# A transformer layer whose expert stage mixes dense products and row gathers: 64 of its 384 dense tokens change sides for the first table

## The chip, the cores and the metric

The kernel runs on one core of one Trainium2 chip. The metric is the device time of one execution in microseconds (us). The engines are TensorE (PE, with its weight loads shown apart as PEld), VectorE (DVE), ScalarE (ACT), GpSimd (POOL) and SyncE (SP, which only issues transfers here); 16 DMA engines move the data.

## The reference, cut to what matters

One layer for 512 latent tokens of width 1024: an attention and gated-delta sublayer, then PEER, a retrieval of single-neuron experts. There are 16384 experts; each token takes 16 of them in each of 8 heads, 128 in all.

```python
s = einsum('phxd,xkd->phxk', q, sub_keys)          # scores against 2 x 128 keys
s_top, i_top = top_k(s, 16)                        # per head and half
cand = s_top[:, :, 0, :, None] + s_top[:, :, 1, None, :]
best, pos = top_k(cand, 16)
expert = i1 * 128 + i2                             # 16 experts per head
gate = softmax(best)
act = gelu(einsum('phkd,pd->phk', u_tab[expert], xt))
y = einsum('phk,phkd->pd', gate * act, v_tab[expert])
```

The tables u_tab and v_tab have 16384 rows of 1024 float32 values, 64 MB each.

## The kernel before, in words

The first part (to about 540 us) computes the mixing sublayer and is not touched. What follows is written in `_peer`. The 512 tokens lie in four slots of 128.

Slots 0 to 2 (ND = 384 tokens) are dense. The 16384 experts are taken in 128 blocks of 128. For each block `t_uload` loads 512 KB of the U table, `t_usplit` (L2099 on ACT, L2101 on DVE) splits it into two float16 halves, `t_u` multiplies it with all 384 tokens (24 matmuls of 384 columns, named 128x384 in the profile), and `t_act` (L2134) takes the Gelu into an activation block. `t_g` (L2190, L2195, L2197) multiplies the block with the gates and splits the product, `t_vsplit` (L2174, L2176) splits 512 KB of the V table, and `t_v` accumulates the output (18 matmuls of 512 columns, 128x512).

The gates of the dense tokens come from `t_gates`: each slot's ranking (`t_top`, `t_slot`) leaves 128 pairs of keys and a gate per token; transposes (L1995), one-hot rows built by DVE (L2023 to L2029, four operations for 16 tokens, 24 such chunks) and small matmuls (128x128) make a full matrix of gates, which ACT copies out (L2041) and a transfer writes to DRAM as `wd` (L2046). `ev_wall` is set when all 24 chunks are written. Only then are `wd` and the V table read, so no product with V can begin before it.

Until then an activation block has to be kept. The blocks come from `acts`: 8 (`acts0`) and 21 (`actsq`) and 6 (`acts1`) before the gates are done, 16 more after. When none is free and `ev_wall` is not set, `t_u` may use one of two spill buffers and park the block in DRAM (`actd`, L2138), at most NSPILL = 20 times; `t_aload` (L2151) reads these back after the wall.

Slot 3 (GSLOT) gathers. `t_gather` (L2267) waits for the slot's ranking and for the wall, and for each of 128 picks gathers 128 rows of U (512 KB, one row for each token); `t_gu` (L2277, two DVE instructions) takes the dot products. Then 128 gathers of V follow, which `t_gv` (L2299) scales and sums. Four row buffers (`grow`) go round, and gather n is held back until dense block (n - 4) * 32 / 100 has its gates.

The order on each engine is fixed when the program is built: every task is a generator with a priority (a lower number goes first), and a planner with a cost for each instruction always takes the ready step that can begin earliest, within a small window the one of the lowest number. U splits have 60.5, the slots' ranking 61 to 61.7, gates 70, 71 and 72 by slot, U and V loads 74 and 73, slot 3's ranking 75.5, gathers 77, their products 78, V products 81. The engines then run their queues in that order and wait on semaphores.

Of the kernel before, what the change touches and what calls it, by code (L numbers as in the profile page):

```python
# [16 lines left out]
F32 = mybir.dt.float32  # L17
# [138 lines left out]
def get(res, n=1):  # L156
    return ("get", res, n)
# [22 lines left out]
def ac(n, p=0, sb=0):  # L180
    return ("ACT", 0.051 + 0.042 * sb + n * 0.833e-3 + 0.093 * p)
# [1512 lines left out]
def _peer(nc, V, A, G, PE, io, dbg, drv, sync, mm, reg, bk, bc, Bump, gp4, at3, obk, h2hl, h2d, x1d, modrow, dp_,  # L1694
          sm, cst, ident, TILE, ev_h2, ev_gdn, ev_attall, ev_odone, stats, bnhalf, moments, fetch):

    ND = 384
    NE = 128
    NCH = ND // 16
    US, GS = 64.0, 16.0  # L1700
# [31 lines left out]
    h2g = reg(170.5, [D])  # L1732
    scr = reg(152.5, [D], BF16)
    ya = [reg(37 + 4 * i, [D]) for i in range(2)]
    grow = Res([reg(69 + 4 * i, [D]) for i in range(4)])
    ust = Res([reg(17 + 4 * i, [KT, 128]) for i in range(3)])
    uhl = Res([(reg(29 + 4 * i, [KT, 128], F16), reg(31 + 4 * i, [KT, 128], F16)) for i in range(2)])
    ohs = Res([[reg(101 + 12 * i + 4 * j, [16, 64, 2], F16) for j in range(3)] for i in range(2)])
# [94 lines left out]
    def t_score(hx, pr, b):  # L1833
        q = yield get(qTs)
        yield ac(256)
        A.activation(q, bk(b, [2, 128]), AF.Copy, scale=1.0 / WS)
        yield put(wqb, b)
        b = yield get(wqb)
        ps = bk(b, [2, 128])
        yield p32(128, 2)  # L1840
        for s in range(2):
            mm(ps[:, s], q[:, s], subk[:, hx % 2], True, True)
        yield put(qTs, q)
        for s in (2 * pr + 1, 2 * pr):
            sc = yield get(scs[s])
            yield ac(128)
            A.activation(sc, ps[:, s % 2], AF.Copy)
            yield ("spawn", t_top(hx, s, sc), 61 + 0.2 * s if s != GSLOT else 75.5)
# [136 lines left out]
    def t_gates(s):  # L1985
        yield ev_pair[s]
        yield ev_qdone
        yield ev_iota
        k = pairs[s]
        ii = k["ii"]  # L1990
        b = yield get(wvb)
        ps = bk(b, [3, 128])
        yield ptr32(3)
        for n in range(3):
            PE.transpose(ps[:, n], ii[:, n].rearrange("p k h -> p (k h)"), ident)  # L1995
        yield put(tks, k)
# [6 lines left out]
        yield ac(256)  # L2003
        A.activation(pT[2], twice(2), AF.Copy, scale=1024.0)
        yield dv(256)
        V.scalar_tensor_tensor(pT[3], twice(2), 1024.0, pT[2], op0=OP.mult, op1=OP.subtract)
        yield ("join",)
        yield put(wvb, b)
        left = [8]
        done = Ev()  # L2010

        def chunk(n):
            tk = slice(n * 16, n * 16 + 16)
            oh = yield get(ohs)
# [12 lines left out]
            V.tensor_tensor(oh[2], oh[1], col(3), op=OP.mult)  # L2027
            yield later(dv(2048, 0, 2))
            V.tensor_tensor(oh[1], oh[1], col(2), op=OP.mult)  # L2029
            yield ("join",)  # L2030
            wb = yield get(wbs)
            for q in range(4):
                b = yield get(wvb)
                ps = bk(b, [4, 128])
                yield p16(128, 8)
                for j in range(4):
                    tok = q * 4 + j
                    mm(ps[:, j], row(0, tok), row(1, tok), j == 0, False)
                    mm(ps[:, j], row(0, tok), row(2, tok), False, j == 3)
                yield later(ac(512))  # L2040
                A.activation(wb[:, :, q * 4:q * 4 + 4], ps.rearrange("p t i -> p i t"), AF.Copy, scale=GS / 1024.0)  # L2041
# [21 lines left out]
    def t_iota():  # L2063
        yield ev_qdone
        yield ev_mem1
        yield dm(128 * 256)
        sync.dma_start(iota.rearrange("p a b -> p (a b)"), io["iota"])
        yield put(ohs, [reg(73 + 4 * j, [16, 64, 2], F16) for j in range(3)])
        yield ("set", ev_iota)
        for s in range(3):  # L2070
            yield ev_pair[s]
        yield put(acts, *acts1)
        for s in range(3):
            yield ev_gated[s]
        yield get(tks, 2)
        yield put(acts, *actr(85, 8))
        yield put(tks, tks_late[0])
        yield ev_pair[3]
        yield put(acts, *acts2)
# [23 lines left out]
            Uw[e] = hl  # L2103
            yield ("set", evU[e])

    actd = dp_.tile([NE, 128, ND], F32, name="actd")
    spill = Res([])
    spilled, ev_spill = [], [Ev() for _ in range(NE)]
    NSPILL = 20

    def t_u():
        for e in range(NE):
            out = not acts.q and ev_wall.t is None and len(spilled) < NSPILL and spill.n
            a = yield get(spill if out else acts)
            Aw[e] = a
            if out:
                spilled.append(e)
            yield evU[e]
            b = yield get(ub)
            for k0 in range(0, KT, 2):  # L2120
                yield later(p16(ND, 6))
# [8 lines left out]
    ev_udone, ev_gall = Ev(), Ev()  # L2130

    def t_act(e, b):
        yield ac(ND)
        A.activation(Aw[e], b[:, 0:ND], AF.Gelu, scale=1.0 / US)  # L2134
        yield put(ub, b)
        if e in spilled:
            yield dm(128 * 4 * ND)
            sync.dma_start(actd[e], Aw[e])  # L2138
            yield put(spill, Aw[e])
            yield ("set", ev_spill[e])  # L2140
        else:
            yield ("set", evA[e])

    def t_aload():

        yield ev_wall
        for e in spilled:
            yield ev_spill[e]
            a = yield get(acts)
            yield dm(128 * 4 * ND)  # L2150
            sync.dma_start(a, actd[e])  # L2151
            Aw[e] = a
            yield ("set", evA[e])

# [26 lines left out]
    def t_g():  # L2181
        for e in range(NE):
# [64 lines left out]
        yield ("set", ev_gall)  # L2247


    ev_gu, ev_ga, ev_gv = Ev(), Ev(), Ev()  # L2250

    def t_gather():
# [7 lines left out]
        for name in ("peer_u", "peer_v"):  # L2260
            for p in range(128):
# [60 lines left out]
    def t_final(s):  # L2322
# [52 lines left out]
    drv.add(t_vsplit(), 75)  # L2375
    drv.add(t_g(), 75)
    drv.add(t_v(), 81)
    drv.add(t_gather(), 77)
    drv.add(t_frows(), 90)
    for s in range(4):  # L2380
# [96 lines left out]
```

## Time and profile before

| | |
|---|---|
| time, median of 3 runs (range) | 1719.27 us (1716.97 to 1719.86) |
| profiled execution, time | 1715.12 us |
| its span, first to last instruction | 1713.3 us |
| busy, PE / DVE / ACT / POOL | 95% / 87% / 48% / 31% of the span |
| DMA | 404.41 MB |
| granted TensorE clock, mean | 0.994 of full speed |

The span is the time between the first and the last instruction of the profiled execution, and every moment below is counted from its start. Busy shares are averages over parts with different limits. The three engines' shares sum to more than 100%, since they work at once; PE's instructions overlap, so a busy PE need not be at its peak.

### The profile page before, as it was taken

What the parts mean: (1) busy time and instruction counts of PE and PEld (TensorE: products, weight loads), DVE (VectorE), ACT (ScalarE), POOL (GpSimd) and SP (SyncE); (2) the same over time, 40 slices, a digit from 0 to 9 for tenths busy, and PEclk for the clock granted to TensorE, in tenths of its full rate; (3) what the DMA queues carried; (4) which work ended last, traced back from release to release, by engine and by line L of the source; (5) the groups of instructions that cost most, each with busy time, mean ns of one, the idle gap of its engine ahead of it and who ended that gap; (6) DMA issues with size and microseconds to landing.
All of it is one profiled execution on the core that took longest, in us unless ns stands there. A gap on an engine that the chain in (4) does not pass through costs nothing.

```text
span 1713.3 us, 29275 instructions
## 1 busy us (share of the span) xinstructions
PE 1624.7 (95%) x10971; PEld 984.9 (57%) x10971; DVE 1483.8 (87%) x2905; ACT 818.0 (48%) x1475; POOL 530.8 (31%) x383
## 2 busy tenths in 40 slices
PE   8889899888998999999999999999999999989997
PEld 2554466787856885677655555555555555534443
DVE  5789985887899999999987789888888988898976
ACT  2645769777543434566543333333333333344441
POOL 0423451433002000000005455555445545554100
PEclk9999999999999999999999999999999999999999
DMA  9546322222134403599989999999999999999852
GB/s 360 185 156 206 120 75 69 77 66 67 41 133 142 142 2 99 159 271 278 276 302 332 355 353 361 365 375 341 361 381 338 369 361 332 328 344 335 327 182 74
DMA packets 157170, 404.41 MB, mean 236 GB/s; under 512 B 12498, under 2 KB 71378, under 8 KB 151906
## 3 DMA queue, kind: packets, MB, share of 16 engines
q1 hardware_dynamic: 120164, 268.30, 45.5%
q0 software_dynamic: 36864, 134.23, 21.4%
q8 instruction: 86, 1.41, 0.3%
q14 instruction: 56, 0.46, 0.1%
HBM read 365.84 MB, written 36.65 MB: 235 GB/s over the span
## 4 chain that ended last, share of the span: by engine, by line
PE 58%; DVE 29%; issue 5%; ACT 4%; DMA 3%; POOL 1%; SPq 0%; DVEq 0%; POOLq 0%; ACTq 0%
PE bank L207 56%; DVE arena L2101 3%; DVE arena L860 2%; DVE arena L2027 2%; DVE arena L2025 1%; DVE arena L2029 1%; DVE arena L1802 1%; DVE arena L1859 1%; DVE arena L1861 1%; DVE arena L2023 1%; DVE arena L1865 1%; DVE arena L1153 1%; DVE arena L1857 1%; DMA arena<-in_peer_v 1%; DVE arena L1863 1%
## 5 line engine op out<-in xcount | busy, mean ns | idle before, releaser
L207 PE MATMUL bank<-arena 128*128 128x512 f16 (+8 forms) x10490 | 1583.4, 311 | 53.6 <-DVE arena L1153 9.5
L207 PEld LDWEIGHTS <-arena 128*128 128x128 f16 x9528 | 836.7, 98 | 620.9 <-issue 29.0
L2267 POOL DMA_INDIRECT arena<-in_peer_u,arena x128 | 179.7, 1404 | 493.1 <-DVE arena L1975 335.5
L2099 ACT ACTIVATE arena<-arena 128x1024 f16<-128x1024 f32 x128 | 135.1, 1056 | 255.2 <-PE bank L207 211.7
L2267 POOL DMA_INDIRECT arena<-in_peer_v,arena x128 | 194.3, 1518 | 170.7 <-DVE arena L2299 151.5
L2174 ACT ACTIVATE arena<-arena 128x1024 f16<-128x1024 f32 x128 | 134.6, 1052 | 123.2 <-PE bank L207 82.4
L2277 DVE SCALAR_TENSOR_TENSOR arena<-arena 128x1024 bf16<-128x1024 f32 x128 | 156.3, 1221 | 40.0 <-DMA arena<-in_peer_u,arena 37.1
L2176 DVE TENSOR_TENSOR arena<-arena 128x1024 f16<-128x1024 f32 x128 | 156.1, 1220 | 28.7 <-ACT arena L2174 28.3
L2299 DVE SCALAR_TENSOR_TENSOR arena<-arena 128x1024 f32<-128x1024 f32 x126 | 160.4, 1281 | 22.2 <-DMA arena<-in_peer_v,arena 22.1
L2101 DVE SCALAR_TENSOR_TENSOR arena<-arena 128x1024 f16<-128x1024 f32 x128 | 156.5, 1222 | 24.5 <-ACT arena L2099 24.5
L207 PEld LDWEIGHTS bank<-arena 128*128 128x128 f32 (+2 forms) x962 | 114.4, 183 | 49.5 <-issue 31.6
L2195 ACT ACTIVATE arena<-arena 128x384 f16<-128x384 f32 x128 | 66.4, 519 | 157.1 <-DVE arena L2190 148.0
L2041 ACT ACTIVATE arena<-bank 128x512 f32<-128x512 f32 x96 | 55.7, 594 | 40.8 <-PE bank L207 39.1
L2190 DVE TENSOR_TENSOR arena<-arena 128x384 f32<-128x384 f32 x128 | 70.6, 552 | 2.0 <-DMA arena<-wd 2.0
L2197 DVE TENSOR_TENSOR arena<-arena 128x384 f16<-128x384 f32 x128 | 70.6, 551 | 1.3 <-ACT arena L2195 1.3
L607 POOL TENSOR_TENSOR arena<-arena 128x512 f32<-128x512 f32 x24 | 38.2, 1591 | 104.5 <-issue 50.1
L2134 ACT ACTIVATE arena<-bank 128x384 f32<-128x384 f32 x128 | 60.9, 476 | 4.8 <-PE bank L207 4.8
L1111 POOL TENSOR_TENSOR arena<-arena 128x512 f32<-128x512 f32 x12 | 18.2, 1520 | 116.9 <-DVE arena L1108 112.7
L1153 DVE TENSOR_TENSOR arena<-bank,arena 128x512 f16<-128x512 f32 x72 | 48.6, 683 | 4.9 <-PE bank L207 4.7
L860 DVE SCALAR_TENSOR_TENSOR arena<-arena 128x770 f32<-128x770 f32 (+1 forms) x48 | 48.6, 1014 | 0.2
L1572 POOL TENSOR_TENSOR arena<-arena 128x1024 f32<-128x1024 f32 x4 | 11.3, 2830 | 118.3 <-DVE arena L1570 103.7
L1161 ACT ACTIVATE arena<-bank 128x512 f16<-128x512 f32 x60 | 36.4, 611 | 14.7 <-PE bank L207 10.5
(258 smaller groups left out, 1398.5 us busy)
## 6 DMA issues: line engine op xcount, KB each, us to landing
arena<-in_peer_ut SPq DMA_DIRECT2D x128, 512.0 KB
arena<-in_peer_v SPq DMA_DIRECT2D x128, 512.0 KB
arena<-in_w_ada SPq DMA_DIRECT2D x24, 1024.0 KB
wd<-arena SPq DMA_DIRECT2D x24, 1024.0 KB
arena<-wd SPq DMA_DIRECT2D x16, 1536.0 KB
arena<-in_w_int SPq DMA_DIRECT2D x21, 512.0 KB
arena<-in_wq SPq DMA_DIRECT2D x16, 512.0 KB
arena<-in_x SPq DMA_DIRECT2D x8, 512.0 KB
```

Of the source, the lines that this page charges most:

```text
L207: PE.matmul(out, lhsT=l, rhs=r, start=start, stop=stop, skip_group_check=True)
L860: V.scalar_tensor_tensor(acc[:, :n], raw[:, j:j + n], convw[:, ci, j:j + 1], acc[:, :n], op0=OP.mult, op1=OP.add)
L2099: A.activation(hl[0], Ud[e], AF.Copy, scale=US)
L2101: V.scalar_tensor_tensor(hl[1], Ud[e], US, hl[0], op0=OP.mult, op1=OP.subtract)
L2174: A.activation(hl[0], Vd[e], AF.Copy)
L2176: V.tensor_tensor(hl[1], Vd[e], hl[0], op=OP.subtract)
L2190: V.tensor_tensor(a3, a3, Wr[w][:, :, e % 8], op=OP.mult)
L2195: A.activation(g[0], a, AF.Copy)
L2197: V.tensor_tensor(g[1], a, g[0], op=OP.subtract)
L2267: G.indirect_dma_start(out=r, out_offset=None, in_=io[name], in_offset=bass.IndirectOffsetOnAxis(ap=gidx[:, p:p + 1], axis=0))
L2277: V.scalar_tensor_tensor(scr, r, 1.0, h2g, op0=OP.mult, op1=OP.mult, accum_out=gact[:, p:p + 1])
L2299: V.scalar_tensor_tensor(y, r, gact[:, p:p + 1], y, op0=OP.mult, op1=OP.add)
```

## The change

Of slot 2, tokens 64 to 127 (columns 320 to 383 of the dense 384) no longer take part in the dense product with U. Their U rows are gathered instead: 64 tokens with 128 experts each are 8192 rows, 64 gathers of 128 rows, each gather serving the 64 tokens twice (two halves of the partitions). `t_hyb` makes the indices when slot 2 is ranked, `t_hu` takes the 64 dot products, the Gelu, and multiplies it into slot 2's gates, so that for these tokens the matrix of gates holds gate times activation already. Slot 2's gates wait for that (`ev_hyb`). In `t_g` these 64 columns are copied by ACT where the other 320 are multiplied by DVE. The product with V stays as it was.

The gathers of slot 3 now wait for `ev_hdot` (the 64 new gathers done) instead of the wall and the spill buffers; those of U are no longer held back by the dense blocks, those of V by block p * 100 / 128. Slot 3's ranking gets 70.5 and 70.6, behind the gates of slot 0 and ahead of those of slots 1 and 2. There is one set less of one-hot rows (two for three) and one row buffer less before the wall. NSPILL becomes 36.

```diff
+    HT, HS = 64, 2
+    NU = ND - HT
+    NHJ = 128 * HT // 128
+    NCU = NU // 16
...
-    grow = Res([reg(69 + 4 * i, [D]) for i in range(4)])
+    grow = Res([reg(73 + 4 * i, [D]) for i in range(3)])
...
+        if s == HS:
+            yield ev_hyb
...
-        yield put(ohs, [reg(73 + 4 * j, [16, 64, 2], F16) for j in range(3)])
...
-    NSPILL = 20
+    NSPILL = 36
...
-                        mm(b[:, 0:ND], Uw[e][j][:, k], h2hl[i][:, k, 0:ND], k == 0 and n == 0, k == KT - 1 and n == 2)
+                        mm(b[:, 0:NU], Uw[e][j][:, k], h2hl[i][:, k, 0:NU], k == 0 and n == 0, k == KT - 1 and n == 2)
...
-            yield dv(ND)
-            V.tensor_tensor(a3, a3, Wr[w][:, :, e % 8], op=OP.mult)
+            yield later(ac(HT, 0, 1))
+            A.activation(a3[:, NCU:], Wr[w][:, NCU:, e % 8], AF.Copy)
+            yield dv(NU)
+            V.tensor_tensor(a3[:, 0:NCU], a3[:, 0:NCU], Wr[w][:, 0:NCU, e % 8], op=OP.mult)
+            yield ("join",)
...
+    def t_hyb():
+        yield ev_pair[HS]
+        yield ev_mem1
+        yield ev_qdone
...
+        for n in range(NHJ):
+            r = yield get(grow)
+            yield pl(450)
+            G.indirect_dma_start(out=r, out_offset=None, in_=io["peer_u"],
+                                 in_offset=bass.IndirectOffsetOnAxis(ap=hidx[:, n:n + 1], axis=0))
+            yield ("spawn", t_hu(n, r), 69)
+
+    def t_hu(n, r):
+        yield dm(128 * 4096)
+        yield dv(1024, 1)
+        V.scalar_tensor_tensor(scr, r, 1.0, h2g, op0=OP.mult, op1=OP.mult, accum_out=hact[:, n:n + 1])
+        yield put(grow, r)
...
+        yield ("set", ev_hdot)
+        yield ac(NHJ, 0, 1)
+        A.activation(hact, hact, AF.Gelu)
...
+        yield ("set", ev_hyb)
...
-        yield ev_wall
-        yield get(spill, 2)
+        yield ev_hdot
...
-                n = p + (128 if name == "peer_v" else 0)
-                if n > 4:
-                    yield evG[min((n - 4) * 32 // 100, NE - 1)]
+                if name == "peer_v":
+                    yield evG[min(PACE0 + p * PACE // 128, NE - 1)]
...
+    PACE0, PACE = 0, 100
...
-        drv.add(t_slot(s), 61.1 + 0.2 * s if s != GSLOT else 75.6)
+        drv.add(t_slot(s), 61.1 + 0.2 * s if s != GSLOT else 70.6)
```

## Rows read from the trace of the kernel before

**Rows 1.** The page: busy time of each engine; DMA's share in 40 slices of the span.

```profile
PE 1624.7 (95%) x10971; PEld 984.9 (57%) x10971; DVE 1483.8 (87%) x2905; ACT 818.0 (48%) x1475; POOL 530.8 (31%) x383
...
DMA  9546322222134403599989999999999999999852
```

**Rows 2.** Stretches: length; busy PE, PEld, DVE, ACT, POOL; clock, DMA share, GB/s.

```profile
600.00:735.00 135.00, 129.91 (x992) 91.72 (x993) 135.00 (x549) 58.38 (x113) 0.00 (x0) 1.00 0.32 98
735.00:842.40 107.40, 104.26 (x1036) 75.66 (x1033) 107.33 (x101) 70.34 (x117) 0.00 (x0) 1.00 0.95 274
...
872.30:1600.00 727.70, 723.16 (x3845) 375.59 (x3845) 627.73 (x804) 281.80 (x381) 373.71 (x256) 1.00 0.95 347
1600.00:1713.30 113.30, 102.42 (x475) 46.23 (x473) 85.87 (x157) 37.17 (x49) 0.21 (x1) 0.97 0.50 176
735.00:1713.30 978.30, 957.49 (x5532) 514.38 (x5529) 848.10 (x1213) 401.04 (x564) 373.93 (x256) 0.99 0.89 319
600.00:1713.30 1113.30, 1087.40 (x6520) 606.10 (x6520) 983.10 (x1761) 459.42 (x676) 373.93 (x256) 1.00 0.83 292
```

**Rows 3.** The chain that ended last: start, length, work, around the wall.

```profile
842.52 6.42 PE bank L207 x50
849.64 5.36 DMA wd<-arena
855.07 8.73 DMA arena<-wd
...
872.34 588.98 PE bank L207 x3202
```

**Rows 4.** Groups of VectorE by line: count, busy us, mean ns, idle before. First 600 to 842.4.

```profile
L2101 DVE SCALAR_TENSOR_TENSOR arena<-arena 128x1024 f16<-128x1024 f32 x38 | 46.7, 1228 | 0.0
```

**Rows 5.** The same groups in 842.4 to 897.1, where slot 3's ranking ends.

```profile
L2101 DVE SCALAR_TENSOR_TENSOR arena<-arena 128x1024 f16<-128x1024 f32 x9 | 11.0, 1219 | 1.4 <-ACT arena L2099 1.4
L2176 DVE TENSOR_TENSOR arena<-arena 128x1024 f16<-128x1024 f32 x5 | 6.1, 1220 | 0.5 <-ACT arena L2174 0.5
```

**Rows 6.** Stretches again: the time of rows 5, phase three's middle.

```profile
842.40:897.10 54.70, 52.40 (x312) 29.96 (x313) 50.36 (x196) 25.65 (x35) 0.00 (x0) 0.97 0.85 292
900.00:1400.00 500.00, 500.00 (x2722) 266.01 (x2721) 426.61 (x564) 190.35 (x258) 264.36 (x190) 1.00 0.97 358
```

**Rows 7.** A stretch of 10 us.

```profile
1090.00:1100.00 10.00, 10.00 (x56) 5.23 (x54) 8.75 (x14) 4.49 (x6) 4.50 (x4) 1.00 1.03 413
```

**Rows 8.** VectorE's timeline: start, length, line; when one instruction follows another.

```profile
910.16 1.22 DVE L2277 SCALAR_TENSOR_TENSOR arena<-arena 128x1024 bf16<-128x1024 f32 x1
...
911.42 1.22 DVE L2277 SCALAR_TENSOR_TENSOR arena<-arena 128x1024 bf16<-128x1024 f32 x1
...
912.57 1.22 DVE L2101 SCALAR_TENSOR_TENSOR arena<-arena 128x1024 f16<-128x1024 f32 x1
913.71 1.22 DVE L2277 SCALAR_TENSOR_TENSOR arena<-arena 128x1024 bf16<-128x1024 f32 x1
```

**Rows 9.** TensorE's groups by form, in 642 to 872.3, where U products begin.

```profile
L207 PE MATMUL bank<-arena 128*128 128x384 f16 x1056 | 187.8, 327 | 4.8 <-DVE arena L2101 2.7 <-ACT arena L2134 2.1
```

**Rows 10.** The same in 1150 to 1200.

```profile
L207 PE MATMUL bank<-arena 128*128 128x512 f16 x125 | 28.1, 379 | 0.0
L207 PE MATMUL bank<-arena 128*128 128x384 f16 x144 | 24.4, 326 | 0.0
```

**Rows 11.** The same in 1650 to 1700.

```profile
L207 PE MATMUL bank<-arena 128*128 128x512 f16 x233 | 50.5, 379 | 0.0
```

**Rows 12.** The page's groups, whole kernel: slot 3's U products and the gates' product.

```profile
L2277 DVE SCALAR_TENSOR_TENSOR arena<-arena 128x1024 bf16<-128x1024 f32 x128 | 156.3, 1221 | 40.0 <-DMA arena<-in_peer_u,arena 37.1 <-issue 1.3 <-DVE arena L2101 0.7
...
L2190 DVE TENSOR_TENSOR arena<-arena 128x384 f32<-128x384 f32 x128 | 70.6, 552 | 2.0 <-DMA arena<-wd 2.0
```

**Rows 13.** The page's DMA queues: the gathers' packets, MB, share of 16 engines' span.

```profile
q0 software_dynamic: 36864, 134.23, 21.4%
```

**Rows 14.** Line views: duration ns, first and last start; parked blocks, the gates' transposes.

```profile
L2138 SPq DMA_DIRECT2D actd<-arena x5: 427/980/4819, 830.7 to 881.3; - x5
...
L1995 PE MATMUL bank<-arena x9: 272/273/332, 646.2 to 733.1; 128*128 128x128 f32 x9
```

More of the change, by code (lines that the diff above doesn't have):

```diff
@@ L1734, in _peer @@
     ya = [reg(37 + 4 * i, [D]) for i in range(2)]
-    grow = Res([reg(69 + 4 * i, [D]) for i in range(4)])
+    grow = Res([reg(73 + 4 * i, [D]) for i in range(3)])
+    hidx, hstage = [reg(kb, [NHJ]).bitcast(I32) for kb in (4.5, 4.75)]
+    hact, hmove = reg(5, [NHJ]), reg(5.25, [NHJ])
     ust = Res([reg(17 + 4 * i, [KT, 128]) for i in range(3)])
@@ L1847, in t_score @@
             A.activation(sc, ps[:, s % 2], AF.Copy)
-            yield ("spawn", t_top(hx, s, sc), 61 + 0.2 * s if s != GSLOT else 75.5)
+            yield ("spawn", t_top(hx, s, sc), 61 + 0.2 * s if s != GSLOT else 70.5)
         yield put(wqb, b)
@@ L2002, in t_gates @@
             A.activation(pT[n], twice(n), AF.Copy)
[L2003 to L2006, printed above, removed]
+        for tk, up in ((slice(0, 128), 1024.0),) if s != HS else ((slice(0, 128 - HT), 1024.0), (slice(128 - HT, 128), GS)):
+            yield ac(256)
+            A.activation(pT[2][:, tk], twice(2)[:, tk], AF.Copy, scale=up)
+            yield later(dv(256))
+            V.scalar_tensor_tensor(pT[3][:, tk], twice(2)[:, tk], up, pT[2][:, tk], op0=OP.mult, op1=OP.subtract)
         yield ("join",)
@@ L2013, in chunk @@
             tk = slice(n * 16, n * 16 + 16)
+            down = GS / 1024.0 if s * 8 + n < NCU else 1.0
             oh = yield get(ohs)
@@ L2040, in chunk @@
                 yield later(ac(512))
-                A.activation(wb[:, :, q * 4:q * 4 + 4], ps.rearrange("p t i -> p i t"), AF.Copy, scale=GS / 1024.0)
+                A.activation(wb[:, :, q * 4:q * 4 + 4], ps.rearrange("p t i -> p i t"), AF.Copy, scale=down)
                 yield put(wvb, b)
@@ L2104, in t_usplit @@
             yield ("set", evU[e])
-    actd = dp_.tile([NE, 128, ND], F32, name="actd")
+    actd = dp_.tile([NE, 128, NU], F32, name="actd")
     spill = Res([])
     spilled, ev_spill = [], [Ev() for _ in range(NE)]
-    NSPILL = 20
+    NSPILL = 36
     def t_u():
@@ L2120, in t_u @@
             for k0 in range(0, KT, 2):
-                yield later(p16(ND, 6))
+                yield later(p16(NU, 6))
                 for k in range(k0, k0 + 2):
                     for n, (i, j) in enumerate(PASS):
-                        mm(b[:, 0:ND], Uw[e][j][:, k], h2hl[i][:, k, 0:ND], k == 0 and n == 0, k == KT - 1 and n == 2)
+                        mm(b[:, 0:NU], Uw[e][j][:, k], h2hl[i][:, k, 0:NU], k == 0 and n == 0, k == KT - 1 and n == 2)
             yield ("join",)
@@ L2132, in t_act @@
     def t_act(e, b):
-        yield ac(ND)
-        A.activation(Aw[e], b[:, 0:ND], AF.Gelu, scale=1.0 / US)
+        yield ac(NU)
+        A.activation(Aw[e][:, 0:NU], b[:, 0:NU], AF.Gelu, scale=1.0 / US)
         yield put(ub, b)
         if e in spilled:
-            yield dm(128 * 4 * ND)
-            sync.dma_start(actd[e], Aw[e])
+            yield dm(128 * 4 * NU)
+            sync.dma_start(actd[e], Aw[e][:, 0:NU])
             yield put(spill, Aw[e])
@@ L2149, in t_aload @@
             a = yield get(acts)
-            yield dm(128 * 4 * ND)
-            sync.dma_start(a, actd[e])
+            yield dm(128 * 4 * NU)
+            sync.dma_start(a[:, 0:NU], actd[e])
             Aw[e] = a
@@ L2247, in t_tailmem, with t_grow @@
         yield ("set", ev_gall)
+    ev_hyb, ev_hdot = Ev(), Ev()
+    h_left = [NHJ]
+    def t_hyb():
+        yield ev_pair[HS]
+        yield ev_mem1
+        yield ev_qdone
+        ii = pairs[HS]["ii"]
+        up = slice(128 - HT, 128)
+        for dst, j in ((hstage, 0), (hidx, 1)):
+            i1, i2 = [ii[up, x].rearrange("p k h -> p (k h)")[:, j * NHJ:(j + 1) * NHJ] for x in range(2)]
+            yield dv(NHJ)
+            V.scalar_tensor_tensor(dst[up], i1, 128.0, i2, op0=OP.mult, op1=OP.add)
+        yield dm(HT * 256)
+        sync.dma_start(hidx[0:HT], hstage[up])
+        t = TILE[HS]
+        for q in range(2):
+            yield later(dm(HT * 4096))
+            sync.dma_start(h2g[q * HT:(q + 1) * HT], h2d[(t + 1) * 128 - HT:(t + 1) * 128, :])
+        yield ("join",)
+        for n in range(NHJ):
[9 more added lines that the diff above has]
+        yield put(grow, r)
+        h_left[0] -= 1
+        if h_left[0]:
+            return
+        yield ("set", ev_hdot)
+        yield ac(NHJ, 0, 1)
+        A.activation(hact, hact, AF.Gelu)
+        yield dm(HT * 256)
+        up = slice(128 - HT, 128)
+        sync.dma_start(hmove[up], hact[0:HT])
+        g = pairs[HS]["ii"][up, 2].rearrange("p k h -> p (k h)")
+        for src, j in ((hact, 1), (hmove, 0)):
+            gj = g[:, j * NHJ:(j + 1) * NHJ]
+            yield dv(NHJ)
+            V.tensor_tensor(gj, gj, src[up], op=OP.mult)
+        yield ("set", ev_hyb)
     ev_gu, ev_ga, ev_gv = Ev(), Ev(), Ev()
+    def t_grow():
+        yield ev_wall
+        yield get(spill, 2)
+        yield put(grow, reg(69, [D]))
     def t_gather():
@@ L2260, in t_gather @@
         for name in ("peer_u", "peer_v"):
+            if name == "peer_v":
+                yield ev_wall
             for p in range(128):
-                n = p + (128 if name == "peer_v" else 0)
-                if n > 4:
-                    yield evG[min((n - 4) * 32 // 100, NE - 1)]
+                if name == "peer_v":
+                    yield evG[min(PACE0 + p * PACE // 128, NE - 1)]
                 r = yield get(grow)
@@ L2377, in _peer @@
     drv.add(t_v(), 81)
+    drv.add(t_hyb(), 60)
+    drv.add(t_grow(), 77)
     drv.add(t_gather(), 77)
```

## Prediction

> **What bounds the kernel now.** I read the shares of the whole span first, then the span in stretches, then the chain, then groups by form in single stretches. The shares say that PE and DVE are both nearly full [rows 1]. The stretches show that they are full in different places, and that DMA is a third. From 600 to 842.4 DVE has no gap at all while PE works 234 of 242 us [rows 2]: ranking and one-hot rows set this stage, and U products run beside them. From 872.3 on PE is the full one: the chain is one unbroken run of 589 us of matmuls [rows 3], and DVE has 86% of that stretch [rows 2]. Between the two lies the wall: last gate matmuls at 842.5, gates written from 849.6, read back from 855.1, first product with V at 872.3 [rows 3], 30 us after DVE's last one-hot row. The DMA digits are 9 in nearly every slice after that [rows 1], and 735 to 842.4 already has a share of 0.95 [rows 2]. So phase two (to the wall) is DVE's, phase three PE's, and in both DMA has 3 to 5% to spare.
>
> **TensorE: what is saved.** In the tail, 233 matmuls of 512 columns take 50 us, 0.2146 each [rows 11]. In 1150 to 1200, 125 of these are 26.8 us, and 144 of 384 columns share the other 23.2: 0.161 each [rows 10], in proportion to their columns. With 320 columns I take 0.134. All 128 x 24 U matmuls then save 3072 x 0.027 = 83 us. That counts only where PE is full.
>
> **VectorE: what is added before the wall.** Back to back, a dot product with its accumulator read begins 1.26 us after the one before, and a U split takes 1.14 [rows 8]. The 64 new dot products cost 64 x 1.26 = 80.6 us, the index and gate arithmetic some 1.5 (an estimate: six instructions of the length of small ones). In `t_g` DVE saves 64 of 384 columns of 552 ns [rows 12], at most 92 ns x 128 = 12 us, after the wall. ACT takes the copy of those columns instead; it is busy 282 of 728 us there [rows 2], so I cost it at nothing, and at 0.2 us a block if it were exposed, 26 us in all.
>
> Slot 3's ranking moves ahead of the gates of slots 1 and 2. In 842.4 to 897.1 DVE is busy 50.4 us [rows 6]; 9 U splits (10.3) and 5 V splits (5.7) are not ranking [rows 5], nor are five blocks of gate products, ten instructions of about 0.5, 5 us. The other 29 us are slot 3's ranking, which lay behind the last one-hot row and now lies before it. They hid beside the wall's transfers; now they are on DVE's path to the wall.
>
> When does DVE finish the one-hot rows? Before: 242.4 us from 600 on, of which 38 splits [rows 4] are 43.3, so 199.1 of everything else. After: 199.1 + 29 + 80.6 + 1.5 = 310 plus the U splits of the time. How many there are is set by activation blocks: 35 are there before the wall, and 36 may be parked, so 71 blocks (and two splits ahead): 73 x 1.14 = 83 us. The last one-hot row comes at 600 + 393 = 993, 151 us later than before. From there to V's first product it was 30 us [rows 3], a few of them U matmuls among the last gate matmuls; with 28, V begins at 1021.
>
> **TensorE waits for that.** From 642, where U begins, to 872.3 PE did 1056 U matmuls [rows 9], 44 blocks, 170 us, and 60 us of gate matmuls and gaps. In the new 379 us it can do 71 blocks, 71 x 24 x 0.134 = 228, plus the same 60: about 90 us idle, because no activation block is left from about 910 on. This is where the saving goes: PE is 83 us shorter and waits 90 longer.
>
> From V's first product on, before: 84 blocks of U x 24 x 0.161 = 325, V 128 x 18 x 0.2146 = 494, together 819 of the 841 us to the end; 22 are lost, the last layer norms among them. After: 57 x 24 x 0.134 = 183, V 494, the same 22: 699. 1021 + 699 = 1720, 7 us more than the span of 1713.3. This is the bound by PE alone.
>
> **DMA: what is added.** All gathers together took 21.4% of the span, 367 us for 256 [rows 13], 1.43 us of all 16 engines each; 64 more are 92 us. Only 5 blocks were parked [rows 14]; 36 of 160 KB, written and read, add 9.8 MB, 27 us at 358 GB/s [rows 6]. Nothing is taken away, since every U block is still loaded. The new gathers can't begin before slot 2 is ranked, at about 733, when the last of the transposes of its pairs began [rows 14]. From 735 DMA was busy 0.89 of 978 us [rows 2], 871; now 871 + 92 + 27 = 990. At that pace DMA ends at 735 + 990 = 1725 if it never idles. It must: in the last 113 us it was idle half of the time [rows 2], and the last products and layer norms, some 40 us, have nothing left to load. That gives 1765. The other end: 10 us at 413 GB/s and a share of 1.03 [rows 7], 401 GB/s for a full DMA, against 369 in the middle of phase three [rows 6]; at 401 the 990 shrink to 911, DMA could end at 1686, and PE's 1720 stands. The stretch of 500 us, with the same mix of loads and gathers, is nearer to what is added than 10 us that may hold a larger transfer, so I go more than half of the way from 1720 to 1765: a span of 1745.
>
> The Trainium skill, "DMA: Bandwidth & Descriptors", Specifications, gives a core about 358 GB/s from HBM. The 500 us of this trace have that very mean, but the 10 us of rows 7 are above it, so it is no hard limit here. By it the 355 MB (312 before, 33.5 of gathers, 9.8 of blocks) would be 992 us from 735, with the same 40 a span of 1767.
>
> Two small edits: with two sets of one-hot rows DVE may wait for PE once in a chunk, 0 to 1 us x 24; I take 0, since splits and dot products are there to fill in. POOL's issues are covered: POOL did nothing from 600 to 897 [rows 2, 6].
>
> The sum was made against the profiled span; that execution's time was 1.8 us longer, and the median of the runs 4 us longer than that. A span of 1745 then is 1747 to 1751, and I say 1748.
>
> **The rivals.** *The wall is paid for by idle DVE time, and PE's saving is kept* (faster). Once no activation block is free, U splits stop; if dot products of slot 3 are done in that lull and behind the last one-hot row, phase three has fewer gathers, DMA room, and loses less than 22 us. For it: DVE and DMA are both nearly as full as PE in phase three, so unloading it helps. Against it: DVE has no gap before the wall. It decides below V's first product at 1010. With that at 1000 and 12 us less lost: 1000 + 687 = 1687; I say 1690. Chance 0.24.
>
> *New dot products wait in DVE's queue for rows that land late.* DVE waited 37.1 us on slot 3's U rows, 0.29 us for each of 128 [rows 12], at an 86% load with four buffers. Behind a waiting dot product stand U splits and one-hot rows, which PE and the wall wait for. With three buffers and a full DMA 0.29 to 1 us for each of 64 puts the wall 19 to 64 us later: 1764 to 1809, and 1785 in the middle. Chance 0.15.
>
> *The losses balance the saving* (no change): PE's 1720 holds and phase three loses 7 us less. Chance 0.08. That the U products don't get shorter with fewer columns is excluded by rows 10 and 11.
>
> **How the numbers follow.** My forecast, slower with V late and DMA full, has 0.53, and a range of its own of 1724 to 1775. A measurement of this kernel tells 0.2%, 3.4 us, from no change. Slower: 0.53 + 0.15 = 0.68; same 0.08; faster 0.24. The range of 8 in 10 goes from 1690, which leaves out half of the faster case, to 1795, which leaves out the worse part of the late rows.
>
> **What would show it.** Right: U matmuls of 0.134 us; V's first product near 1021; PE with some 90 us of gaps between 900 and 1020 that end on activation blocks or on gates; 36 blocks parked; a DMA share above 0.95 from 735 to 1650. Wrong: V before 1000, PE without gaps before the wall, fewer than 36 parked, or a phase three that runs above 385 GB/s without PE gaps.

## The result, and the profile after

The changed kernel takes 1826.91 us (median; 1823.59 to 1836.49) beside 1718.34 us before: a ratio of 1.0641, interval 1.0597 to 1.0684. The forecast was 1748 us, slower by 1.7%. The direction is right; the loss is nearly four times as large, and the time lies outside the range. The profiled execution took 1829.39 us and its span is 1827.4 us.

The page after, beside [rows 1]: busy TensorE, then the granted clock and DMA's share in 40 slices of 45.7 us.

```profile
PE 1578.8 (86%) x10971; PEld 996.2 (55%) x10971; DVE 1552.5 (85%) x3038; ACT 827.4 (45%) x1605; POOL 616.4 (34%) x447
...
PEclk9999999999999999877768899999999999999997
DMA  9546222211335035888979989999999999899992
```

PE is busy 46 us less (1624.7 before) and the span is 114 us longer. The digits of the clock dip in slices 17 to 23, about 730 to 1050 us (and in the last one, around PE's end). The stretches around it, columns as in [rows 2]:

```profile
735.00:950.00 215.00, 106.52 (x855) 78.20 (x853) 178.38 (x371) 56.64 (x92) 92.57 (x67) 0.74 0.84 273
900.00:950.00 50.00, 11.87 (x104) 10.03 (x102) 41.52 (x62) 9.38 (x18) 20.61 (x16) 0.59 0.80 262
950.00:1048.70 98.70, 71.40 (x667) 55.46 (x666) 77.60 (x83) 44.77 (x77) 16.62 (x11) 0.88 1.01 322
1048.70:1700.00 651.30, 632.47 (x3519) 342.14 (x3519) 554.72 (x719) 268.46 (x455) 318.90 (x218) 0.99 0.95 349
...
735.00:1827.40 1092.40, 913.14 (x5501) 521.20 (x5498) 920.25 (x1349) 409.57 (x693) 459.35 (x320) 0.92 0.90 321
```

From 735 to 950 nothing is full: PE works half of the time, DVE 83%, DMA 0.84. Before, the same stage (735 to 842.4) had PE and DVE at 97 and 100% [rows 2]. So this is a stage of waits, and the question is on what. TensorE's waits from 740 to 1048.7 (line and what it waited for; us in total, times, longest):

```profile
PE bank L207 <- DVE arena L2040: 88.3, 11, 31.0
PE bank L207 <- DVE arena L2111: 23.1, 6, 13.5
PE bank L207 <- ACT arena L2144: 11.0, 2, 5.8
PE bank L207 <- ACT arena L2109: 8.9, 1, 8.9
```

L2040 is the last of DVE's four operations of one chunk of one-hot rows (L2029 before), L2111 the U split, L2144 the Gelu that frees a bank. So two thirds of the waiting is gate matmuls without their one-hot rows. Where DVE is meanwhile, its timeline shows (start, length; in brackets its idle time and what ended it):

```profile
763.96 1.22 DVE L2294 SCALAR_TENSOR_TENSOR arena<-arena 128x1024 bf16<-128x1024 f32 x1
765.11 0.08 DVE L2294 DVE_READ_ACCUMULATOR arena<-arena 128x1 f32 x1
768.98 1.22 DVE L2294 SCALAR_TENSOR_TENSOR arena<-arena 128x1024 bf16<-128x1024 f32 x1 [3.79 <-DMA arena<-in_peer_u,arena]
...
772.42 1.23 DVE L2294 SCALAR_TENSOR_TENSOR arena<-arena 128x1024 bf16<-128x1024 f32 x1 [2.21 <-DMA arena<-in_peer_u,arena]
...
780.66 2.35 DVE L2040 TENSOR_TENSOR arena<-arena 128x2048 f16<-128x2048 f16 x2
```

And TensorE's at the same moment:

```profile
781.93 2.29 PE L207 MATMUL bank<-arena 128*128 128x128 f16 x20 [18.07 <-DVE arena L2040]
```

A dot product (L2294) stands at the head of DVE's queue and waits for its gathered rows. Behind it, in the fixed order, stands a chunk of one-hot rows; in PE's fixed order a gate matmul waits for that chunk, and U products behind it can't pass. So the 18.07 us of PE's wait hold 6.0 in which DVE waited for rows (3.79 and 2.21) and 12 in which it worked, on six dot products, which its order puts first, and on the chunk itself. In PE's longest wait, 31.0 us up to 931.3, DVE waited 7.2 for rows. The lines of the new dot products and of their gathers (duration ns, first and last start; idle before; who waited; landing):

```profile
L2294 DVE SCALAR_TENSOR_TENSOR arena<-arena x64: 1204/1224/1227, 751.5 to 939.3; 128x1024 bf16<-128x1024 f32 x64
...
  DMA arena<-in_peer_u,arena: 27.8, 24
who waited for it (us, times):
  POOL arena L2287: 74.2, 32
...
L2287 POOL DMA_INDIRECT arena<-in_peer_u,arena x64: 932/1347/1980, 740.0 to 933.8; - x64
...
DMA to landing us min/median/max: 4.2/5.7/10.6
```

The 64 gathers are issued over 194 us, 3.1 us apart. With three buffers one round is 9.2 us: 5.7 until rows land, then the time until DVE comes to the dot product and frees the buffer, on which POOL waited 74 us. It goes both ways: DVE waits for rows, and the rows' buffers wait for DVE. Slot 2's gates can't begin before the last dot product. Slot 3's gathers follow on the same queue (first and last start), here and, with L2267, before:

```profile
L2334 POOL DMA_INDIRECT arena<-in_peer_u,arena x128: 934/1677/1988, 944.6 to 1391.5; - x128
L2334 POOL DMA_INDIRECT arena<-in_peer_v,arena x128: 932/1327/3278, 1394.2 to 1771.0; - x128
```

```profile
L2267 POOL DMA_INDIRECT arena<-in_peer_u,arena x128: 932/1673/1979, 897.9 to 1233.5; - x128
L2267 POOL DMA_INDIRECT arena<-in_peer_v,arena x128: 932/1344/3083, 1236.3 to 1599.2; - x128
```

They begin 47 us later, when slot 3 is ranked (944), and take 826 us for 701. This stream of slot 3 comes back below. Then comes the wall, beside [rows 3]:

```profile
1009.02 9.27 PE bank L207 x80
1019.88 9.04 DMA wd<-arena
1029.05 9.43 DMA arena<-wd
...
1048.75 24.83 PE bank L207 x142
```

TensorE's groups by form, 642 to 1047.5, beside [rows 9]: what it got done until then.

```profile
L207 PE MATMUL bank<-arena 128*128 128x320 f16 x1392 | 213.6, 310 | 45.9 <-DVE arena L2111 25.9 <-ACT arena L2144 11.0 <-ACT arena L2109 8.9
L207 PE MATMUL bank<-arena 128*128 128x128 f16 x768 | 62.8, 244 | 92.0 <-DVE arena L2040 89.7 <-ACT arena L2052 2.4
```

1392 U matmuls are 58 blocks. Against the forecast:

| | forecast | measured |
|---|---|---|
| one U matmul, us | 0.134 | 0.135 |
| from one dot product to the next, back to back, us | 1.26 | 1.26 |
| last one-hot row | 993 | 1012.4 |
| V's first product | 1021 | 1047.5 |
| U blocks done by then / parked in all | 71 / 36 | 58 / 19 |
| PE idle from 642 to it | 100 (its 90, and 10 of gaps in its 60) | 140 |
| DMA busy, from 735 on | 990 | 983 |
| PE's losses after V's first product | 22 | 61 |

The 0.135 is worked out as in the prediction: 130 matmuls of 512 columns and 164 of 320 share the 50 us from 1150. The 1.26 is the step from 778.24 to 779.50. The 983 is 0.90 of 1092.4. The losses: PE ends at 1807.7, 760 us after V's first product, with 1680 x 0.134 = 225 and 494 of products in them; 41 are lost, and 20 more to the span's end.

So the 107 us between TensorE's sum (1720) and the span (1827.4) are: V's start 27 us later, 13 blocks more left for afterwards (13 x 24 x 0.134 = 42), losses 39 us larger. They make 108.

### The profile page after: what moved, and what is told of

It reads as the page before. It is cut to its first block, busy times and chain, and to the rows that moved or that the text cites. A ratio compares the mean times of both kernels' runs of the same rounds, so it can differ in the third digit from the quotient of the medians.

```text
span 1827.4 us, 29820 instructions
## 1 busy us (share of the span) xinstructions
PE 1578.8 (86%) x10971; PEld 996.2 (55%) x10971; DVE 1552.5 (85%) x3038; ACT 827.4 (45%) x1605; POOL 616.4 (34%) x447
## 4 chain that ended last, share of the span: by engine, by line
PE 29%; DVE 29%; DMA 20%; issue 13%; ACT 4%; POOL 4%; DVEq 0%; SPq 0%; POOLq 0%; ACTq 0%
PE bank L207 28%; DMA arena<-in_peer_u,arena 14%; DMA arena<-in_peer_v,arena 3%; DVE arena L2111 2%; POOL arena L2334 2%; DVE arena L860 2%; DVE arena L2294 1%; DVE arena L1809 1%; DVE arena L2186 1%; DVE arena L2366 1%; DVE arena L2040 1%; DVE arena L1868 1%; DVE arena L2034 1%; DVE arena L1866 1%; DVE arena L2038 1%
## 5 line engine op out<-in xcount | busy, mean ns | idle before, releaser
L207 PE MATMUL bank<-arena 128*128 128x512 f16 (+8 forms) x10490 | 1536.9, 307 | 204.6 <-DVE arena L2040 89.7
L207 PEld LDWEIGHTS <-arena 128*128 128x128 f16 x9528 | 847.8, 100 | 712.4 <-issue 113.1
L2334 POOL DMA_INDIRECT arena<-in_peer_u,arena x128 | 178.4, 1394 | 280.0 <-DVE arena L2344 251.6
L2344 DVE SCALAR_TENSOR_TENSOR arena<-arena 128x1024 bf16<-128x1024 f32 x128 | 156.4, 1222 | 40.6 <-DMA arena<-in_peer_u,arena 39.8
L2287 POOL DMA_INDIRECT arena<-in_peer_u,arena x64 | 89.0, 1390 | 279.9 <-DVE arena L2111 174.2
L2111 DVE SCALAR_TENSOR_TENSOR arena<-arena 128x1024 f16<-128x1024 f32 x128 | 155.9, 1218 | 22.8 <-ACT arena L2109 22.6
L2184 ACT ACTIVATE arena<-arena 128x1024 f16<-128x1024 f32 x128 | 134.3, 1050 | 78.3 <-PE bank L207 44.6
L2294 DVE SCALAR_TENSOR_TENSOR arena<-arena 128x1024 bf16<-128x1024 f32 x64 | 78.2, 1221 | 28.5 <-DMA arena<-in_peer_u,arena 27.8
L2210 DVE TENSOR_TENSOR arena<-arena 128x384 f16<-128x384 f32 x128 | 70.6, 551 | 13.1 <-ACT arena L2208 13.1
L2144 ACT ACTIVATE arena<-bank 128x320 f32<-128x320 f32 x128 | 54.3, 424 | 43.7 <-PE bank L207 31.3
L2202 DVE TENSOR_TENSOR arena<-arena 128x320 f32<-128x320 f32 x128 | 61.9, 483 | 9.5 <-DMA arena<-wd 9.5
```

Source lines behind the costliest of these rows:

```text
L207: PE.matmul(out, lhsT=l, rhs=r, start=start, stop=stop, skip_group_check=True)
L2111: V.scalar_tensor_tensor(hl[1], Ud[e], US, hl[0], op0=OP.mult, op1=OP.subtract)
L2184: A.activation(hl[0], Vd[e], AF.Copy)
L2210: V.tensor_tensor(g[1], a, g[0], op=OP.subtract)
L2287: G.indirect_dma_start(out=r, out_offset=None, in_=io["peer_u"], in_offset=bass.IndirectOffsetOnAxis(ap=hidx[:, n:n + 1], axis=0))
L2294: V.scalar_tensor_tensor(scr, r, 1.0, h2g, op0=OP.mult, op1=OP.mult, accum_out=hact[:, n:n + 1])
```

## The experiments

Two theories stood. **Late rows**: the ring of three buffers holds up the dot products, and they hold up all queues; without that wait the sum of the prediction comes out. **DVE's work**: the dot products, splits and ranking themselves fill DVE until 993 or later, and the waits only show where it was short. A third, **the rest of the change** (ranking ahead, two sets of one-hot rows, slot 3 released early), was costed at little.

**1. Three more row buffers.** They are taken from the activation blocks, of which there are 8 fewer, and slot 3 uses them afterwards.

```diff
+    grow_more = [reg(kb, [D]) for kb in (49, 53, 57)]
...
-    actsq = actr(194.5, 8) + actr(49, 13)
+    actsq = actr(194.5, 8) + actr(61, 5)
...
+            yield put(grow, *grow_more)
```

> Six row buffers for the gathers before the wall instead of three (8 activation blocks fewer). Late rows in a fixed order (the 64 new gathers go round in three buffers, 9.4 us a round, and what stands behind their dot products waits): the 64 dot products take 130 us or less instead of 188, the wall comes some 50 us earlier, time 1765 to 1790. Amount of work (VectorE and DMA simply have more to do): the work is the same, time 1817 to 1837.

1971.39 us, 1.1459 (1.1416 to 1.1501). Both expectations missed. The dot products ran from 751.9 to 851.3, 100 us rather than 188, so the ring is what spaced them. But the planner now put them ahead of everything else:

```profile
735.00:850.00 115.00, 27.08 (x265) 21.22 (x264) 106.17 (x196) 14.11 (x25) 84.77 (x64) 0.63 0.97 343
```

DVE is at 92% and PE at 24%. V began near 1018, some 30 us earlier, but with 45 U blocks done for 58, and later PE stood 149 us at once:

```profile
PE bank L207 <- ACT arena L2210: 156.4, 7, 149.0
```

L2210 is the half of the gates' product that ACT makes. Which of the two, fewer activation blocks or the new order, brings that wait, this kernel doesn't tell. It says that the ring's wait can be moved, and nothing about what it costs.

**2. The planner is told that the new rows land 3.5 us later.** Nothing else changes: the same work in another fixed order.

```diff
+'lLAT': 3.5
...
 def t_hu(n, r):
     yield dm(128 * 4096)
+    yield ("LAT", 0.0)
```

> The planner is told that the rows of the 64 new gathers land 3.5 us later, so that it puts other work of VectorE ahead of their dot products; the work and the buffers are the same. Late rows in a fixed order: VectorE's 28 us of waits for these rows go to under 10, TensorE's 90 us of waits for one-hot rows to under 50, time 1785 to 1815. Amount of work: 1817 to 1837.

1850.67 us, 1.0773 (1.0729 to 1.0816), outside both ranges. TensorE's waits from 740 to 1078:

```profile
PE bank L207 <- DVE arena L2040: 51.8, 13, 14.2
PE bank L207 <- DVE arena L2111: 26.7, 15, 3.9
```

88.3 became 51.8, near the 50 expected; DVE's own waits for rows hardly changed, 24.0 us for 27.8, where under 10 were expected. 36 blocks were parked and 1812 U matmuls (75.5 blocks) done before V, more than the 71 of the forecast, in part because V began 31 us later, near 1079: the dot products took until 980.0 and the last one-hot row came at 1044.6. Even so PE ended at 1789.8, 18 us sooner than in the change (1807.7). The span ended 56 us after it, on slot 3: its gathers come behind the 64 new ones and began at 974.9, and its last product began at 1802.9. The new order spared PE some time and cost slot 3's stream more.

**3. No rows: 61 of the 64 new gathers are left out.** The dot products run on the three buffers filled first, so the activations of those 64 tokens are not the reference's.

```diff
+            if n < 3:
                 G.indirect_dma_start(out=r, ..., in_=io["peer_u"], ...)
...
 def t_hu(n, r):
+        if n < 3:
             yield dm(128 * 4096)
```

> Leaves out 61 of the 64 new gathers: the first three fill the row buffers, all 64 dot products are taken on those, so the gates of 64 tokens are not the reference's. Late rows in a fixed order: without rows to wait for, the 64 products run together, the stage shrinks by about 100 us, time 1700 to 1760. Amount of work: VectorE keeps its 80 us and only DMA gets its 92 us back, time 1780 to 1805.

1811.11 us, 1.0531 (1.0490 to 1.0572): 16 to 19 us better than the change, of the 109 lost, and just above the range for DVE's work. Its one-hot rows' line, and its stretches:

```profile
L2040 DVE TENSOR_TENSOR arena<-arena x24: 1196/1219/1243, 711.8 to 1010.2; 128x2048 f16<-128x2048 f16 x24
```

```profile
735.00:950.00 215.00, 182.43 (x1429) 127.35 (x1427) 203.98 (x390) 89.41 (x141) 7.94 (x4) 0.96 0.64 201
950.00:1042.30 92.30, 54.21 (x474) 44.69 (x473) 71.39 (x80) 33.71 (x61) 30.06 (x18) 0.68 1.00 312
...
1741.40:1808.60 67.20, 0.01 (x1) 0.00 (x0) 48.84 (x99) 5.28 (x5) 12.45 (x10) 0.54 0.49 173
```

Now DVE has 95% of 735 to 950. The dot products are done at 866, and still the last one-hot row comes at 1010: with no row to wait for, DVE's work alone takes that long, 17 us above the forecast's 993. Ten dot products of slot 3 (10 x 1.26 = 12.6 us), which the forecast's sum did not have there, come before that row. The parked blocks (36) and the blocks before V (75) come out as forecast or above. And the last row shows a new end: PE is done at 1741.4, 66 us sooner than in the change, and the span lasts 67 us longer, on slot 3, whose last product begins at 1764.0. So most of what the late rows cost PE does not show in the time here.

**4. No rows, and the last 48 of slot 3's V gathers and products left out too**: is that end slot 3's stream?

```diff
-            for p in range(128):
+            for p in range(80 if name == "peer_v" else 128):
...
-    gv_left = [128]
+    gv_left = [80]
```

> As the run without the new rows, and the last 48 of slot 3's 128 V gathers and their products are left out as well, so that slot 3's output is not the reference's either. If slot 3's stream sets the end there (its last product began 44 us before the end): 1755 to 1775. If the wall and TensorE set it: 1800 to 1812.

1748.69 us, 1.0176 (1.0142 to 1.0210): 62 us less than experiment 3. PE ends at 1738.4, nearly where it did, and the span 11 us later. So slot 3's stream was the end there. Its first gather starts when slot 3 is ranked, at 948 in experiment 3, 945 in the change and 898 before.

**5. Short dot products: all gathers stay, each dot product takes 16 of 1024 columns** (so the 64 tokens' activations are not the reference's).

```diff
-        yield dv(1024, 1)
+        yield dv(16, 1)
-        V.scalar_tensor_tensor(scr, r, 1.0, h2g, ...)
+        V.scalar_tensor_tensor(scr[:, 0:16], r[:, 0:16], 1.0, h2g[:, 0:16], ...)
```

> The changed kernel with all 64 new gathers, but each dot product takes 16 of 1024 columns, so the activations of 64 tokens are not the reference's; VectorE is spared some 70 us. If VectorE's work alone sets the wall: last one-hot row near 940, time 1745 to 1765. If the ring of three buffers alone sets it: it stays near 1010, time 1815 to 1835. If both lie close together, as the run without rows suggests (1010 there too): between, 960 to 990, time 1770 to 1810.

1822.87 us, 1.0581 (1.0558 to 1.0605): 67 us of DVE's work gone, and the time is hardly better. The lines of the dot products, the one-hot rows and the U matmuls before V, then two stretches:

```profile
L2294 DVE SCALAR_TENSOR_TENSOR arena<-arena x64: 156/175/238, 749.7 to 925.4; 128x16 bf16<-128x16 f32 x64
...
L2040 DVE TENSOR_TENSOR arena<-arena x24: 1182/1220/1269, 712.4 to 982.8; 128x2048 f16<-128x2048 f16 x24
...
L207 PE MATMUL bank<-arena 128*128 128x320 f16 x1176 | 187.0, 318 | 72.6 <-DVE arena L2111 33.0 <-ACT arena L2109 32.6 <-ACT arena L2144 6.9
```

```profile
735.00:950.00 215.00, 105.81 (x898) 77.85 (x896) 130.22 (x389) 60.91 (x103) 85.50 (x70) 0.74 0.86 284
950.00:1018.50 68.50, 45.00 (x387) 34.05 (x386) 48.35 (x54) 26.31 (x46) 15.90 (x11) 0.88 1.02 343
```

DVE works 61% of the stretch and the dot products still take 176 us, 2.8 apart. With DVE out of the way the rows alone (landing after 7.1 us here) keep V's start at 1018.5, 29 us sooner than in the change. But 1176 U matmuls, 49 blocks, are done by then for 58, and 9 x 24 x 0.134 = 29 us, so PE ends no sooner (1821.1, in a profiled execution of 1834.0). It waited for U splits now; what held these up was not taken apart.

**6. Neither: experiments 3 and 5 together.** The shorter U product stays.

> Both left out: 61 of 64 new gathers, and 1008 of 1024 columns of each new dot product. What stays is the shorter product with U and the rest of the change. Two limits: with both gone the last one-hot row comes at 900 to 920, as without the hybrid. If TensorE's 83 us are then kept: 1690 to 1705, against 1775 without the hybrid. If slot 3's stream or VectorE takes them: 1740 to 1770.

1733.28 us, 1.0085 (1.0065 to 1.0106). The last one-hot row comes at 919.2 and V begins at 954. Removing the rows gained 1.1% (1.0641 to 1.0531), removing the dot products' work 0.6%, both 5.6%. So neither theory alone accounts for the loss: one limit lies right behind the other, and either alone looks harmless. PE's end tells the two apart better than the time: 1807.7 in the change, 1741.4 without rows, 1821.1 with short dot products, 1709.8 with both. In experiment 3 slot 3's stream hid PE's gain, and DVE's work bears on that too: with it gone slot 3 is ranked sooner and its gathers begin at 857 rather than 948.

**7. The rest of the change without the exchange**: all 384 tokens stay dense.

```diff
-    NU = ND - HT
+    NU = ND
...
-        if s == HS:
-            yield ev_hyb
...
-        yield ev_hdot
+        yield ev_qdone
...
-    drv.add(t_hyb(), 60)
```

> The rest of the change alone: all 384 tokens dense in the product with U, no new gathers; slot 3's ranking early, its gathers before the wall, three row buffers, two sets of one-hot rows, 36 blocks parked at most, the new pace for V's gathers. Late rows or amount of work, both with the cost in the 64 new gathers: 1705 to 1745. If the moved ranking and the released gathers cost as much: 1770 or more.

1775.42 us, 1.0321 (1.0291 to 1.0351). I had taken the rest for nearly free. DVE's groups from 800 to 905, before the last one-hot row (899.6; 841 before), show why:

```profile
L2340 DVE SCALAR_TENSOR_TENSOR arena<-arena 128x1024 bf16<-128x1024 f32 x13 | 15.8, 1218 | 0.1
```

These are 13 dot products of slot 3, 12 of them before that row. Its gathers no longer wait for the wall; with its ranking ahead they start at 819, and their products go before gates that the wall needs.

**8 to 10. The parts of the rest, one by one.** Ranking ahead in the kernel before; experiment 7 with the ranking back in its place; the kernel before with two sets of one-hot rows.

```diff
 rank_early (before):   75.5 -> 70.5, 75.6 -> 70.6
 rank_late (exp. 7):    70.5 -> 75.5, 70.6 -> 75.6
 two_sets (before):    -yield put(ohs, [reg(73 + 4 * j, [16, 64, 2], F16) for j in range(3)])
```

> The kernel before with one edit: slot 3's ranking gets 70.5 and 70.6. If what stands ahead of the one-hot rows moves the wall one for one: the last one-hot row 25 to 30 us later, but TensorE goes on with parked blocks, time 1718 to 1735. If this edit is all of the 57 us of the run without the new gathers: 1760 to 1780.

> The run without the new gathers, with slot 3's ranking back behind the gates (75.5 and 75.6): what is left are the released gathers of slot 3, three row buffers, two sets of one-hot rows. If the ranking made the 57 us: 1718 to 1730. If the buffers, the one-hot sets or the release made them: 1750 to 1780.

> The kernel before with two sets of one-hot rows instead of three, nothing else. If the set is what moved the last one-hot row from 841 to 853 in the run with the late ranking: 850 to 856 here, time 1718 to 1730. If it is covered by splits and ranking, as the prediction took it: 1713 to 1721.

Ranking ahead alone: 1726.45 us, 1.0042 (1.0021 to 1.0064), though the last one-hot row is 43 us later (884.7): 14 parked blocks filled PE until then. Ranking late: 1731.28, 1.0082 (1.0055 to 1.0108), last one-hot row at 852.6. Two sets alone: 1737.67, 1.0095 (1.0078 to 1.0111), as much as all that rank_late loses. The prediction had priced them at 0 to 24 us and taken 0. In two_sets the last one-hot row is 17 us later, and PE waits once, at the wall:

```profile
PE bank L207 <- ACT arena L2173: 18.6, 1, 18.6
```

L2173 is ACT's half of the V split. The parts, 0.4 and 0.8%, make 3.2% together: late gates by two sets, late gates by ranking, and only the early ranking and the released gathers together let slot 3's dot products in before the wall (its gathers begin at 930.5 in rank_early, 891.5 in rank_late, both behind V's start, and 819.5 in experiment 7). From rank_late to experiment 7 the last one-hot row moves 47 us; ranking (29) and 12 dot products (15) are 44.

**11. The exchange without the early slot 3**: its ranking, gathers and pace as before. Two sets of one-hot rows and three row buffers stay.

```diff
-    70.5, 70.6
+    75.5, 75.6
...
+        yield ev_wall
...
-                if name == "peer_v":
-                    yield evG[min(PACE0 + p * PACE // 128, NE - 1)]
+                n = p + (128 if name == "peer_v" else 0)
+                if n > 4:
+                    yield evG[min((n - 4) * 32 // 100, NE - 1)]
```

> The change with slot 3 as before: ranked behind the gates, its gathers behind the wall and held to the old pace; the 64 new gathers stay. If the work ahead of the wall sets the time: the wall comes some 30 us earlier than with the whole change, 1780 to 1810. If slot 3's stream of 256 gathers sets the end (it then starts and ends later): 1830 or more. If the hybrid by itself pays: under 1715.

1840.26 us, 1.0712 (1.0684 to 1.0739), slower than the whole change. V begins at 1041, 7 us earlier, with 60 blocks done; but slot 3's stream now runs from 1015 to 1792 (945 to 1779 in the change) and ends the span 55 us after PE (1783.1). So the early start of slot 3, dear without the exchange, pays with it.

**12. The saving free of charge**: the kernel before, with only the U product cut to 320 columns; the other 64 tokens' activations are left out.

```diff
-                        mm(b[:, 0:ND], Uw[e][j][:, k], h2hl[i][:, k, 0:ND], ...)
+                        mm(b[:, 0:NU], Uw[e][j][:, k], h2hl[i][:, k, 0:NU], ...)
```

> The kernel before with the saving alone: the product with U covers 320 columns, the activations of 64 tokens are left out (their gates go on in their place), nothing is added ahead of the wall. If TensorE's 83 us are kept in full: 1635 to 1645. If VectorE, DMA and slot 3's stream, held to the dense blocks' pace, give only part: 1660 to 1700. If nothing: 1710 or more.

1682.49 us, 0.9776 (0.9760 to 0.9793): 38 us of the 83. Its stretches from V's start on:

```profile
883.40:1600.00 716.60, 704.94 (x3912) 381.81 (x3910) 626.29 (x825) 305.35 (x516) 349.48 (x242) 0.99 0.95 353
1600.00:1682.00 82.00, 47.41 (x212) 20.68 (x210) 67.95 (x124) 15.50 (x24) 20.23 (x15) 0.80 0.59 205
```

PE ends at 1650.4, 52 us earlier than before, and the span 32 us after it: slot 3's stream ends at 1638.7 and the layer norms come after. Slot 3 ended at 1610.4 before, at no cost behind PE. That is the next limit as soon as PE has less to do.

Along three kernels the ratios make one sum (experiment 6 still has 3 of the new gathers and 64 short dot products):

| step | ratio to before | us |
|---|---|---|
| the rest of the change (7) | 1.0321 | +57 |
| with the shorter U product (6) | 1.0085 | -42 |
| with rows and dot products (the change) | 1.0641 | +94 |

## Why the prediction was right in direction and wrong in size

**What held.** The U matmul's price; DMA's total (983 us for 990); that the wall moves behind the 64 dot products and the ranking, and that PE's saving doesn't pay for it; the last one-hot row, within 17 us where no row is late (experiment 3). DMA's share above 0.95 from 735 on did not hold before 950, where it is 0.84, and the 25 us that the forecast added to PE's 1720 for a full DMA are not among the 107. By its own sum the direction rested on these 25 and on 7 us of PE's bound, so that it is right is in part luck. The Trainium skill's 358 GB/s ("DMA: Bandwidth & Descriptors", Specifications), by which the prediction had a span of 1767, agrees with the 349 over the 651 us after the wall; from 1150 to 1300 the trace has 367, so here too it is no hard limit.

**The step that failed**: "In the new 379 us it can do 71 blocks [...] about 90 us idle, because no activation block is left". It took PE's work before the wall to be limited by buffers alone, as if PE could do U products whenever it was free. It can't: gate matmuls stand in its queue among them, and these wait for one-hot rows, which stand behind dot products, which wait for gathered rows. 58 blocks were done and 19 parked; 88 of 135 us of waiting from 740 on end on one-hot rows. Experiment 3 puts the blocks (75) and the 36 parked ones back by leaving out only the rows, with V's start within 5 us of where it was and those waits at 36 us, which shows the cause of the missing blocks; experiment 2 does so by the order alone, with a later wall. This is the mechanism of the rival with 0.15, "rows that land late". Its own price, 0.29 to 1 us for each row, was near (27.8 us in all for 64 is 0.43); and its wall, 19 to 64 us later, holds with 27. Its time, 1764 to 1809, does not: what it lacked is that such waits also keep PE from filling the time, so that 13 blocks (42 us) are left over.

V's 27 us and the blocks' 42 are 69 us that PE lost before V. 40 are idle (140 for 100). The other 29 are busy time: PE is busy 266 us from 642 to V, where its work at the prices of the sum is 237. 95 U and 211 gate matmuls of that stretch began at the lower clock level, 0.267 us each for 0.136 and 0.107 for 0.056 from start to start in the trace, which makes some 23 us (an estimate from these counts). The sum had PE's full price throughout. In experiment 3 the same count makes 24, so it does not separate the two.

The last one-hot row, some 20 us late, is a balance of errors: 52 U splits for 73 (24 us less), 38 us of idle DVE (28 on rows) where the sum had none, and six dot products of slot 3 (8).

**Terms mis-sized.** Losses after the wall, 22 for 61: beside DMA the forecast took PE as the only bound there and had no term for slot 3's stream. Experiments 3, 4, 11 and 12 show slot 3's stream as the end as soon as it starts later or PE ends sooner; in the change its last product is at 1778.8 (1610.4 before), just ahead of PE's end. Where that stream was the end, 43 to 46 us followed its last product, and where PE was, 11 followed PE's end; by these the change would end near 1823 by slot 3 and 1819 by PE, and it ends at 1827. So the 107 us, summed along PE, have a second account of nearly the same length beside them, and sparing PE alone would not have won them back, as in experiment 3. Two sets of one-hot rows, 0 for 0.95%. The ranking, 29 us on DVE's path, was right as work (43 us with what came with it) and too dear as time in the kernel before, 0.4%.

**The rival on the other side**, the wall paid by idle DVE time, falls with experiment 3: even with no row to wait for, V begins at 1042.

**Not settled.** After the wall PE loses 28 to 54 us in the kernels with the shorter U product (28 in experiment 4, 29 in u320, 41 in the change, 48 in experiment 2, 54 in experiment 5; 178 in experiment 1, with its wait of 149) against 11 before PE's end in the kernel before. Part are waits on the gates' product (19.1 and 4.6 us on its two halves in the change); what is late ahead of those was not taken apart. Nor was the 149 us wait of six_bufs, nor why slot 3's 128 gathers of U take 447 us for 336.

## What to carry to other kernels

Price the exchange in the stage where it must be paid, per unit: a token moved saves PE 83 / 64 = 1.30 us wherever PE is full, and costs DVE 1.26 us in a stage where DVE was full already, so by these prices there was next to nothing to win here even with rows that are always there. Before a new step with a late input goes into a fixed order, count what stands behind it on its own engine, and then what stands behind that on the next one; a free engine can't use its time if its next instruction waits. When one suspected limit is removed and little happens, remove the next one with it before calling the first harmless, and read the end of each stream beside the time: in experiment 3 PE was done 66 us sooner, and another stream hid most of it.

## What was not expected of the hardware

A gather of 128 rows (512 KB) landed after 4.2 us at best, 5.7 in the middle and 10.6 at worst, in one stage with a DMA share of 0.84; three buffers then give one gather in 3.1 us, where six, in another order, gave one in 1.7 (740.1 to 844.9 for 64).

The granted clock fell from 1.00 (600 to 735) to a mean of 0.74 in 735 to 950, and 0.59 in 900 to 950, where PE worked 11.87 of 50 us; so for most of those 50 us it was at the lower of its two levels, 1.2 GHz of 2.4. With PE full again it is 0.99. In experiment 3, with PE busy 85% of 735 to 950, it stays at 0.96. What the lower level costs shows on 32 gate matmuls of one chunk: 3.57 us from 931.28 at a granted clock of 0.50, 1.96 us from 954.90 at 1.00. What it cost the kernel by itself was not tried.
